# Five of the sixteen column units of the first channel-mix product done in seven block products

## The chip, the cores and the metric

The kernel runs on one core of one Trainium2 chip. The metric is the device time of one execution in microseconds, the median of several runs; lower is better.

## The reference, cut to what matters

The reference is a two-layer encoder trunk on 512 frames of width 1024. The change sits in the channel mix at the end of each layer:

```python
h2 = rmsnorm(x, norm2_g[i])
x = x + jnp.square(jax.nn.relu(h2 @ w_ff1[i] + b_ff1[i])) @ w_ff2[i] + b_ff2[i]
```

`w_ff1` is 1024 x 4096 and `w_ff2` is 4096 x 1024, all in float32. Ahead of it come the combined input projection, two recurrent branches, their merge and the output product `x + merged @ w_out`. Behind it comes the gated per-layer embedding.

## The kernel before, in words

**Products.** Activations lie transposed, features on the 128 partitions and the 512 frames along the free axis. Every float32 operand is split into a high and a low part of type fp32r (`split`: ScalarE copies the high part, VectorE subtracts to get the low part), and a product is three matmuls: high by high, high by low, low by high. `t8` makes one output tile of 128 columns by 512 frames out of eight blocks of the contraction: 24 matmuls, 512 wide.

**Seven products.** A `PAIR` unit is a product of 256 output columns, done as a two-by-two block product in seven block products instead of eight (`run_pair`, `PRODUCTS`). Each of the seven, P1 to P7, is four blocks by three matmuls, 256 wide: 84 matmuls in all. It needs sums of the activation quarters (`operand_sums`, or `pair_operand` for the hidden tiles) and sums of the weight blocks, t1 to t4 (`MADE`). P1 and P5 use the weight piece A, P6 and P2 the piece B, P3 and P7 the piece C, P4 the piece D. P4 of a unit is put off: `later` holds it until `flush`, which stands in the next unit, behind P5 of a pair or behind the fourth block of a `t8`. Before the change the pairs are the retention queries and keys, part of the gates, and the second channel-mix product `w_ff2`; its sixteen units a layer are called `o00` to `o33`.

**Sums of weights.** t1 and t3 are formed in DRAM: `step` issues on GpSimd's queue one copy DMA of 256 KB or one accumulating DMA, and `steps` lists them in the order of `groups`. A credit counter paces them: each unit gives SHARE or LATER times its time, less its loading time (`TIME`), and a step takes STEP = 1.13. A step waits for the last matmul that was written when it was issued (`cur["mm"]`). For the `w_ff2` pairs t2 and t4 are made in SBUF, by two adds of 512 columns on VectorE (L438 and L441).

**Weights on their way.** SyncE loads raw pieces into four buffers (`fill_raws`), and `prep_next` splits them two or so pieces ahead of their product. The order of the instructions on each engine is that of the source, moved by the tile scheduler's priorities; evictions marked `ahead` go first.

**The channel mix.** `ff1(b, p)` makes 256 hidden columns with two `t8` tiles (`f00` to `f33`), multiplies by the norm's factors `n2.b` on VectorE, applies Relu and Square on ScalarE, and forms the quarters' sums. `ff_order` gives the order: f00 f01 f02 f03 f10, o00 to o03, f11 f12 f13 f20, o10 to o13, f21 f22 f23 f30, o20 to o23, f31 f32 f33, an embedding unit, o30 to o33. The norm's factors come from a chain behind f00's first tile: `finish` sums on TensorE, GpSimd raises to the power, `spread` brings the factors to all partitions. Ahead of this stand the eight tiles of `w_out` (`wo`), each followed by a norm tile (`n2.tile`).

Of the kernel before, what the change touches and what calls it, by code (L numbers as in the profile page):

```python
# [42 lines left out]
P = 128  # L43
# [35 lines left out]
def ff_order():  # L79

    seq = [("f", 0, p) for p in range(4)]
    for b in range(3):
# [4 lines left out]

PRODUCTS = {"P1": ("A", 0, 0), "P5": ("A", 1, 4), "P2": ("B", 0, 2), "P6": ("B", 1, 5), "P3": ("C", 0, 6),  # L90
            "P7": ("C", 1, 3), "P4": ("D", 0, 1)}

PIECE = {"A": ("B11", "t1"), "C": ("B22", "t3"), "B": ("B21",), "D": ()}

GIVEN = ("B11", "B12", "B21", "B22")
MADE = {"t1": ("B12", "B11"), "t3": ("B12", "B22"), "t2": ("t1", "B22"), "t4": ("t2", "B21")}
# [8 lines left out]
HALVES = [(WIDE[x][0], u) for x, u in TURNS]  # L105

SOON = ("w_in", 0, CGM + 2 * P)
STEP, SHARE, LATER = 1.13, 0.75, 0.63
TIME = {"PAIR": (9.9, 3.9), "WIDE": (5.45, 2.7)}


def parts_of(u):
# [8 lines left out]
def is_wide(g):  # L121
    return g[1][:2] in ("rv", "rw")


def is_gate(g):
    return g[1][:2] == "rw"


def MADE_OF(g):

    return ("t1", "t3", "t2", "t4") if is_gate(g) else ("t1", "t3", "t2") if is_wide(g) else ("t1", "t3")


def groups():


    g = {}
    for i in range(L):
        def rqk(h):
            return [("w_in", 0, c + k * 256) for k in (h, h + 1) for c in (CRQ, CRK)]  # L140

        g[i, "rv0"] = [("w_in", 0, CRV)]
        g[i, "rqk0"] = rqk(0)
        g[i, "gm"] = [("w_in", 0, CGM + 256 * p) for p in (2, 3)]
        g[i, "rw0"] = [("w_in", 0, CRG)]
        g[i, "rv2"] = [("w_in", 0, CRV + 1024)]
        g[i, "rqk2"] = rqk(2)
        g[i, "rw2"] = [("w_in", 0, CRG + 1024)]
        g[i, "gr"] = [("w_in", 0, CGR + 256 * p) for p in range(4)]
        for b in range(4):  # L150
            g[i, f"ff{b}"] = [("w_ff2", b * 1024, 256 * p) for p in range(4)]
    return g


def unit_list(i):
# [36 lines left out]
    full("w_in", CGM, 0, 2, 3)  # L192
    mqk(2)
    mo(1)
    v(CV + 512)
    mqk(3)
    mo(2)
    full("w_in", CGM, 0, 3, 4)
    mo(3)
    u.append(("WIDE", (i, "rv0"), 0))  # L200
    full("w_bm", 0, 0, 0, 4)
    rqk(0)
    for p in (2, 3):
        pair("gm", p - 2)
        full("w_bm", 0, 0, 2 * p, 2 * p + 2)
    rqk(1)
    u.append(("WIDE", (i, "rw0"), 0))
    u.append(("WIDE", (i, "rv2"), 0))
    rqk(2)
    full("w_br", 0, 0, 0, 4)  # L210
    rqk(3)
    full("w_br", 0, 0, 4, 8)
    u.append(("WIDE", (i, "rw2"), 0))
    for p in range(4):
        pair("gr", p)
        full("w_br", 0, 1024, 2 * p, 2 * p + 2)
    full("w_out")

    def pairs(seq):
        for kind, b, p in seq:  # L220
            if kind == "f":
# [12 lines left out]

def build(ctx, tc, ins, out):
# [120 lines left out]
    def next_unit():  # L356
        n = at["unit"]
        at["unit"] += 1
        tick(units[n][0])
        return n  # L360


    order = [(n, x) for n, u in enumerate(units) for x in parts_of(u)]
    place = {x: k for k, x in enumerate(order)}
    loads = [(n, x) for n, x in order if x != "D" and (x not in (("t4", 0), ("t4", 1)) or is_gate(units[n][1]))]
    raws, pieces, kept = {}, {}, {}
    formed = {}

# [7 lines left out]
    def fill_raws(most=RAWS + 1):  # L376
        while at["load"] < len(loads) and len(raws) + len(kept) < most:
            n, x = loads[at["load"]]
            r = None
            if n in cur["room"] and cur["more"] not in raws:  # L380
                cur["more"] = n, x
                r = cur["low"].tile([P, UN], F32, name=f"wr{at['load']}", tag="wrx", bufs=1)
            elif len(raws) - (cur["more"] in raws) >= RAWS:
                break
            raws[n, x] = r = r or wpool.tile([P, UN], F32, name=f"wr{at['load']}", tag="wr", bufs=RAWS)
            if x:
                _, g, p = units[n]
                assert made.get((g, x[1] if is_wide(g) else p)) == 2 * len(MADE_OF(g)), (g, p, made, at["unit"])
                if is_wide(g):
                    in_order("load", nc.sync.dma_start(r, block(g, x[0])[x[1]]))  # L390
                else:
                    for k, y in enumerate(PIECE[x]):
                        in_order("load", nc.sync.dma_start(r[:, k * Q:(k + 1) * Q], block(g, y)[p]))
            elif units[n][0] == "IF":
                eng = nc.sync if n else nc.scalar
                eng.dma_start(r[:, 0:64], ins["wif"][n * L // NU])
            else:
                w = ins["wstream"][at["whole"]]
                for c in halves(n):
                    in_order("load", nc.sync.dma_start(r[:, c], w[:, c]))  # L400
                at["whole"] += 1
            at["load"] += 1

    def prep_next():
# [24 lines left out]
        else:  # L429
            in_order("prep", *split(r[:, :w], *out_))  # L430
        pieces[n, x] = out_
        if wide and is_gate(units[n][1]):
            pass
        elif x == "A" or wide and x[0] == "t2":
            kept[n, x] = r
# [27 lines left out]
    def t8(act, name):  # L463

        _, wh, wl = unit("T8")
        o = ps(name)
        for k in range(KT):
            s = slice(k * P, (k + 1) * P)
            mm3(o, wh[:, s], wl[:, s], act[0][k], act[1][k], k == 0, k == KT - 1)
            if k == 3:  # L470
                flush()
                pace()
        return o

# [90 lines left out]
    def pair_tiles(name, act, consume, y=None, then=None):  # L565
# [4 lines left out]
        def done(x, o):  # L570
            with ahead():
                evict(x, o)
            if then and x == "P2":
                then()
            if x == "P4":
                consume(y)

# [183 lines left out]
    def values(i, nm, act, rc, bv_ap, n_, mid=None):  # L761
# [4 lines left out]
        for u in range(4):  # L766
# [5 lines left out]
            for kk in range(2):  # L772
                k = 2 * u + kk
                s = slice(kk * T, (kk + 1) * T)
                for j in range(NT):
                    js = slice(j * P, (j + 1) * P)
                    te.matmul(o[j], act[0][k][:, js], wh[:, s], start=(k == 0), stop=False)
                    te.matmul(o[j], act[0][k][:, js], wl[:, s], start=False, stop=False)
                    cur["mm"] = te.matmul(o[j], act[1][k][:, js], wh[:, s], start=False, stop=(k == KT - 1))
        vh = [cur["low"].tile([P, 576], F32R, name=f"{nm}vh{j}", tag="vh", bufs=NT) for j in range(NT)]  # L780
        vl = [cur["low"].tile([P, 576], F32R, name=f"{nm}vl{j}", tag="vl", bufs=NT) for j in range(NT)]
        for j in range(NT):
# [169 lines left out]
    for i in range(L):  # L952
# [160 lines left out]
        def r_attend(h, pt, vv, g=None):  # L1113
# [7 lines left out]
            def each(j):  # L1121
# [2 lines left out]
                c = hv[:, j:j + 1]  # L1124
                gp.tensor_scalar(c, mv[:, j, 1:2], EPS, None, OP.add)
                gp.tensor_tensor(c, c, nhalf[:, 0:1], OP.pow)
                if g and j:
                    r_gate(norm, g, j - 1)

            attend(nm, pt, vv[0], vv[1], 0, 512, num, each)  # L1130
            return norm
# [165 lines left out]
        gs = m_gates(0, xa, n1)  # L1297
        xn_tile(4)
        gm_tile(2, xa, n1)
        xn_tile(5)  # L1300
        m_back(0, gs, num)
        xn_tile(6)
        xn_tile(7)
        xa_pool.release()
        xs_pool = phase(f"xs{i}", act_side)
        shift(xs_pool, act_side, True)
# [50 lines left out]
        yr = acts(cur["br"], f"l{i}yr0")  # L1357
        r_out(0, num[0], yr)
        num = r_attend(1, pt, vv, g)
        r_gate(num, g, NT - 1)  # L1360
        vv = rv_vals(2, lambda: r_out(1, num[0], yr))
        qk = r_qk(2)

# [26 lines left out]

            pair_tiles(f"l{i}gr{p}", xs, consume, then=then)

        gr_gates(0, lambda: r_gate(num, g, NT - 1))
        r_out(3, num[0], yr)
        for c in range(KT):
            if c and c % 2 == 0:
# [26 lines left out]
            gp.dma_start(x[c], x_src[c])  # L1423
        n2_pool = phase(f"n2{i}", act_side)
        n2 = Norm(f"l{i}n2", i, "g2", acts(n2_pool, f"l{i}n2"))
        for c in range(KT):
# [11 lines left out]
        def ff1(b, p):  # L1438
# [5 lines left out]
            def evac(d, o):  # L1444
                a = st[:, d * T:(d + 1) * T]
                ve.tensor_tensor(a, o, n2.b, OP.mult)
                ac.activation(a, a, AF.Relu, bias=bcol(i, "bf1", 8 * b + 2 * p + d))
# [53 lines left out]
        for kind, b, p in first:  # L1501
# [9 lines left out]
            ff1(b, p)  # L1511
        n2_pool.release()
        n3_pool = phase(f"n3{i}", act_side)
        n3 = Norm(f"l{i}n3", i, "g3", acts(n3_pool, f"l{i}n3"))
# [237 lines left out]
```

## Time and profile before

| what | value |
|---|---|
| median of 3 runs | 2329.46 us (2328.98 to 2332.13) |
| the profiled execution | 2331.78 us, span 2330.1 us |
| TensorE | 2313.3 us busy, 99% of the span, granted clock 0.999 |
| VectorE, ScalarE, GpSimd | 1709.6, 1217.6 and 497.2 us busy |
| DMA | 422.15 MB, mean 181 GB/s |

The span runs from the first to the last instruction; the remaining 1.7 us of the execution's time lie around it. The busy time of matmuls is modelled from pipelined records, so how closely matmuls follow each other is read from their start times. A row of the view by windows gives the busy time of each engine in a stretch with its instruction count; a row of the timeline gives start, duration, engine, line, operation and tiles.

### The profile page before, as it was taken

How to read it: one execution, taken by the hardware profiler on the slowest of the kernel's cores; microseconds unless marked ns; L12 is line 12 of the kernel's file. 1: busy time of each engine (PE TensorE's matmuls, PEld its weight loads, DVE VectorE, ACT ScalarE, POOL GpSimd, SP SyncE). 2: the span in 40 equal slices, each digit the busy share in tenths (PEclk: the TensorE clock that was granted, in tenths of full speed). 3: DMA queues.
4: the chain of work that ended last, by engine and by line, in shares of the span. 5: the costliest groups of instructions: out<-in, count | busy, mean ns of one | idle time of the engine just before them, and what ended most of it. 6: DMA issues, size and time to landing. Idle time of an engine off the chain costs nothing.

```text
span 2330.1 us, 34559 instructions
## 1 busy us (share of the span) xinstructions
PE 2313.3 (99%) x12992; PEld 2021.4 (87%) x12992; DVE 1709.6 (73%) x2594; ACT 1217.6 (52%) x1731; POOL 497.2 (21%) x778
## 2 busy tenths in 40 slices
PE   9999999999999999999999999999999999999998
PEld 8888889888888898899888888988888988998997
DVE  7878767886765577678778777778767656776785
ACT  6756434644554445445557564445446445445464
POOL 3222422223123311112422221111121130000012
PEclk9999999999999999999999999999999999999999
DMA  6666997787688776776766668766766852433441
GB/s 202 166 167 157 285 256 212 212 231 212 203 221 231 176 195 174 183 189 177 197 174 168 154 171 233 203 190 193 199 201 185 215 173 96 127 109 96 136 123 55
DMA packets 154121, 422.15 MB, mean 181 GB/s; under 512 B 20880, under 2 KB 24336, under 8 KB 153952
## 3 DMA queue, kind: packets, MB, share of 16 engines
q1 hardware_dynamic: 97504, 257.99, 34.3%
q0 software_dynamic: 41040, 134.51, 26.7%
q10 hardware_dynamic: 15408, 27.43, 3.5%
q8 instruction: 102, 1.67, 0.3%
q14 instruction: 67, 0.55, 0.1%
HBM read 400.97 MB, written 140.51 MB: 232 GB/s over the span
## 4 chain that ended last, share of the span: by engine, by line
PE 90%; DVE 5%; issue 2%; ACT 1%; DMA 1%; POOL 1%; ACTq 0%; DVEq 0%; POOLq 0%; SPq 0%
PE l0f L459 3%; PE l1f L459 3%; PE l1f L460 2%; PE l0f L460 2%; PE l0f L461 2%; PE l1f L461 2%; PE l0br L459 1%; PE l1br L459 1%; PE l1br L460 1%; PE l1br L461 1%; PE l0br L460 1%; PE l0br L461 1%; PE l0pg L459 1%; PE l0bm L459 1%; PE l0pg L460 1%
## 5 line engine op out<-in xcount | busy, mean ns | idle before, releaser
L285 ACT ACTIVATE wh<-wr 128x1024 fp32r<-128x1024 f32 (+1 forms) x223 | 231.5, 1044 | 262.4 <-issue 62.9
L286 DVE TENSOR_TENSOR wl<-wr,wh 128x1024 fp32r<-128x1024 f32 (+1 forms) x221 | 271.8, 1232 | 49.7 <-ACT wh L285 49.3
L285 ACT ACTIVATE wh_B<-wr 128x1024 fp32r<-128x1024 f32 x108 | 114.4, 1059 | 177.2 <-PE l0br L460 15.7
L286 DVE TENSOR_TENSOR wl_B<-wr,wh_B 128x1024 fp32r<-128x1024 f32 x108 | 131.9, 1221 | 51.8 <-ACT wh_B L285 51.7
L459 PE MATMUL l1f<-l1n2h,wh 128*128 128x512 f32 x256 | 99.8, 390 | 0.0
L459 PE MATMUL l0f<-l0n2h,wh 128*128 128x512 f32 x256 | 99.8, 390 | 0.0
L461 PE MATMUL l0f<-l0n2h,wl 128*128 128x512 f32 x256 | 99.7, 389 | 0.0
L461 PE MATMUL l1f<-l1n2h,wl 128*128 128x512 f32 x256 | 99.7, 389 | 0.0
L460 PE MATMUL l0f<-l0n2l,wh 128*128 128x512 f32 x256 | 99.6, 389 | 0.0
L460 PE MATMUL l1f<-l1n2l,wh 128*128 128x512 f32 x256 | 99.6, 389 | 0.0
L285 ACT ACTIVATE wh_D<-wr 128x512 fp32r<-128x512 f32 x60 | 37.9, 632 | 113.1 <-DVE wr L441 49.2
L285 ACT ACTIVATE wh_C<-wr 128x1024 fp32r<-128x1024 f32 x60 | 63.4, 1056 | 61.5 <-issue 8.3
L285 ACT ACTIVATE wh_t<-wr 128x1024 fp32r<-128x1024 f32 x56 | 59.4, 1060 | 66.8 <-PE l1g2va L554 6.0
L286 DVE TENSOR_TENSOR wl_t<-wr,wh_t 128x1024 fp32r<-128x1024 f32 x56 | 68.1, 1219 | 25.9 <-ACT wh_t L285 25.2
L286 DVE TENSOR_TENSOR wl_C<-wr,wh_C 128x1024 fp32r<-128x1024 f32 x60 | 74.8, 1247 | 16.3 <-ACT wh_C L285 15.8
L285 ACT ACTIVATE wh_A<-wr 128x1024 fp32r<-128x1024 f32 x60 | 63.1, 1052 | 40.8 <-PE l1f L460 6.7
L286 DVE TENSOR_TENSOR wl_A<-wr,wh_A 128x1024 fp32r<-128x1024 f32 x60 | 73.2, 1221 | 12.0 <-ACT wh_A L285 11.4
L673 POOL TENSOR_TENSOR l1n3sum<-l1n3sum,l1n3sq 128x512 f32<-128x512 f32 x6 | 9.3, 1546 | 330.7 <-ACT l1n3sum L665 309.8
L286 DVE TENSOR_TENSOR wl_D<-wr,wh_D 128x512 fp32r<-128x512 f32 x60 | 41.4, 690 | 25.7 <-ACT wh_D L285 24.5
L461 PEld LDWEIGHTS l0f<-l0n2h,wl 128*128 128x128 f32 x256 | 48.1, 188 | 10.2
L461 PEld LDWEIGHTS l1f<-l1n2h,wl 128*128 128x128 f32 x256 | 48.1, 188 | 10.1
L460 PEld LDWEIGHTS l0f<-l0n2l,wh 128*128 128x128 f32 x256 | 48.1, 188 | 9.8
(4990 smaller groups left out, 8428.5 us busy)
## 6 DMA issues: line engine op xcount, KB each, us to landing
wr<-wstream SPq DMA_DIRECT2D x219, 512.0 KB, 4.4
wr<-wpairs SPq DMA_DIRECT2D x180, 256.0 KB, 3.5
wr<-wwide SPq DMA_DIRECT2D x48, 512.0 KB, 4.5
s3t<-wwide POOLq DMA_DIRECT2D x24, 256.0 KB, 5.5
s6t<-wwide POOLq DMA_DIRECT2D x24, 256.0 KB, 4.9
s15t<-wwide POOLq DMA_DIRECT2D x24, 256.0 KB, 4.4
s18t<-wwide POOLq DMA_DIRECT2D x24, 256.0 KB, 4.1
s0t<-wwide POOLq DMA_DIRECT2D x20, 256.0 KB, 4.1
```

The lines of the kernel that those rows point to most:

```text
L285: a = ac.activation(hi_ap, src, AF.Copy)
L286: return a, ve.tensor_sub(lo_ap, src, hi_ap.bitcast(F32))
L459: te.matmul(o, sh, mh, start=first, stop=False)
L460: te.matmul(o, sh, ml, start=False, stop=False)
L461: cur["mm"] = te.matmul(o, sl, mh, start=False, stop=last)
L673: (add or gp).tensor_tensor(self.sum, self.sum, sq, OP.add)
```

## The change

Five of the sixteen `ff1` units of each layer, f11, f13, f21, f23 and f31, become `PAIR` units of new groups `fp1`, `fp2` and `fp3`. The operand sums that they need (`n2_seven`) are formed behind every second tile of the output product `w_out`, in a new pool of 16 tiles. The weight sum t2 of all channel-mix pairs, old and new, is formed in DRAM in both layers, and t4 too in layer 1, so the adds at L438 go in both layers and those at L441 in layer 1; piece B is then two loads, and piece D of layer 1 is a load. That makes 630 steps on GpSimd's queue where there were 464 (each layer gains 32 or 64 for `w_ff2` and 30 or 40 for the new groups). LATER rises from 0.63 to 0.73, and `pace` is called at two places of a `t8` instead of one and after each `V` unit. Besides, two gate steps of the retention branch move later by one place and three norm tiles (`xn_tile`) earlier.

```diff
+FPAIRS = ((1, 1), (1, 3), (2, 1), (2, 3), (3, 1))
-PIECE = {"A": ("B11", "t1"), "C": ("B22", "t3"), "B": ("B21",), "D": ()}
+PIECE = {"A": ("B11", "t1"), "C": ("B22", "t3"), "B": ("B21", "t2"), "D": ("t4",)}
-STEP, SHARE, LATER = 1.13, 0.75, 0.63
-TIME = {"PAIR": (9.9, 3.9), "WIDE": (5.45, 2.7)}
+STEP, SHARE, LATER = 1.13, 0.75, 0.73
+TIME = {"PAIR": (9.9, 3.9), "WIDE": (5.45, 2.7), "FULL": (9.9, 5.0)}
+def is_full(g):
+    return is_gate(g) or g[0] > 0 and g[1][0] == "f"
+def has_t2(g):
+    return is_full(g) or g[1][0] == "f"
...
+            f = [p for c, p in FPAIRS if c == b]
+            if f:
+                g[i, f"fp{b}"] = [("w_ff1", 0, b * 1024 + 256 * p) for p in f]
             g[i, f"ff{b}"] = [("w_ff2", b * 1024, 256 * p) for p in range(4)]
...
-        if wide and is_gate(units[n][1]):
+        if full(n) or not wide and x in ("A", "C") and has_t2(units[n][1]):
             pass
...
             if k == 3:
                 flush()
+            if k in (2, 5):
                 pace()
...
-                if g and j:
-                    r_gate(norm, g, j - 1)
+                if g and j > 1:
+                    r_gate(norm, g, j - 2)
...
-        xn_tile(5)
+        for k in (5, 6, 7):
+            xn_tile(k)
         m_back(0, gs, num)
-        xn_tile(6)
-        xn_tile(7)
...
-        gr_gates(0, lambda: r_gate(num, g, NT - 1))
+        gr_gates(0, {"P6": lambda: r_gate(num, g, 2), "P2": lambda: r_gate(num, g, 3)})
...
+        def n2_sums(k):
+            v = [tmp(f"l{i}ns{k}{a}") for a in range(2)]
+            for a in range(2):
+                ve.tensor_tensor(v[a], *[t[2 * k + a].bitcast(F32) for t in n2.act], OP.add)
+            operand_sums(f"l{i}ns{k}", v, *[t[2 * k:2 * k + 2] for t in ns])
         for c in range(KT):
             o = t8((mh, ml), f"l{i}wo{c}")
             ve.tensor_tensor(x[c], o, x[c], OP.add)
             n2.tile(c, x[c])
+            if c % 2:
+                n2_sums(c // 2)
...
+            if (b, p) in FPAIRS:
+                def consume(y):
+                    for d in range(2):
+                        evac(d, y[d], SIGN[d])
+                    pair_quarters(st, *hid[b, p])
+                    pair_operand(nm, st, *hid[b, p])
+                pair_tiles(nm, n2_seven, consume, [st[:, d * T:(d + 1) * T] for d in range(2)])
+                return
```

Where the rows below name `wh` and `wl`, these are the high and the low part of a split weight piece (`wh_A` of piece A of a pair, without a letter of a `t8`), `st` is a unit's staging tile, `hl` the low part of its hidden tiles.

On VectorE in layer 0, around unit f11, there stood before:

```order
L1446 TENSOR_TENSOR l0f11st<-l0f_8593,l0n2rb 128x512
L286 TENSOR_TENSOR wl_0_8639<-wr_8487,wh_0_8638 128x1024
L1446 TENSOR_TENSOR l0f11st<-l0f_8642,l0n2rb 128x512
L286 TENSOR_TENSOR wl_0_8684<-wr_8564,wh_0_8683 128x1024
L599 TENSOR_TENSOR l0f11st<-l0f11st 128x512
L600 SCALAR_TENSOR_TENSOR l0f11st<-l0f11st 128x256
L286 TENSOR_TENSOR l0hl_8584<-l0f11st,l0hh_8583 128x768
L601 SCALAR_TENSOR_TENSOR l0f11st<-l0f11st 128x256
```

Now there stands, from the eviction of its product P2 on:

```order
L606 TENSOR_TENSOR l0f11st<-l0f11b,l0f11st 128x256
L304 TENSOR_TENSOR wl_0_8827<-wr_8698,wh_0_8826 128x1024
L610 TENSOR_TENSOR l0f11st<-l0f11c,l0f11st 128x256
L612 TENSOR_TENSOR l0f11st<-l0f11a,l0f11st 128x256
L1485 TENSOR_TENSOR l0f11st<-l0f11st,l0n2rb 128x512
L304 TENSOR_TENSOR wl_A<-wr_8721,wh_A 128x1024
L1485 TENSOR_TENSOR l0f11st<-l0f11st,l0n2rb 128x512
L621 TENSOR_TENSOR l0f11st<-l0f11st 128x512
L1485 TENSOR_TENSOR l0f12st<-l0f_8853,l0n2rb 128x512
L304 TENSOR_TENSOR l0hl_8718<-l0f11st,l0hh_8717 128x768
L622 SCALAR_TENSOR_TENSOR l0f11st<-l0f11st 128x256
L304 TENSOR_TENSOR wl_C<-wr_8744,wh_C 128x1024
```

Three evictions of 256 columns are new, the multiplications by the norm's factors read SBUF instead of the accumulator, and pieces A and C of the next pair, f13, are split among f11's own steps.

On VectorE in layer 0, two tiles of the output product took these rows before:

```order
L1428 TENSOR_TENSOR l0x_7328<-l0wo_7370,l0x_7328 128x512
L286 TENSOR_TENSOR wl_0_7404<-wr_7228,wh_0_7403 128x1024
L655 SCALAR_TENSOR_TENSOR l0n2l_7348<-l0x_7328,bc,l0n2h_7347 128x512
L1428 TENSOR_TENSOR l0x_7329<-l0wo_7407,l0x_7329 128x512
L286 TENSOR_TENSOR wl_0_7443<-wr_7287,wh_0_7442 128x1024
L655 SCALAR_TENSOR_TENSOR l0n2l_7350<-l0x_7329,bc,l0n2h_7349 128x512
```

After the last of these rows there stands now:

```order
L1460 TENSOR_TENSOR l0ns_7503<-l0n2h_7390,l0n2l_7391 128x512
L1460 TENSOR_TENSOR l0ns_7504<-l0n2h_7392,l0n2l_7393 128x512
L633 TENSOR_TENSOR l0ns0u_7507<-l0ns_7503 128x256
L634 TENSOR_TENSOR l0ns0u_7507<-l0ns_7504,l0ns_7503 128x256
L635 SCALAR_TENSOR_TENSOR l0ns0u_7508<-l0ns0u_7507,l0ns_7503 128x256
L636 SCALAR_TENSOR_TENSOR l0ns0u_7508<-l0ns0u_7508,l0ns_7504 128x256
L304 TENSOR_TENSOR l0nsl_7417<-l0ns0u_7507,l0nsh_7409 128x512
L1465 TENSOR_TENSOR l0x_7373<-l0wo_7524,l0x_7373 128x512
```

The operand sums of two tiles add eight VectorE rows (the eighth, a second `nsl` of 512 columns, stands a little further on) ahead of and behind the next tile's addition to `x`.

On GpSimd in layer 1, ahead of the norm's power `l1n2rc`, there stood only the norm's own additions; now steps of the weight sums (`s27t`) stand between them:

```order
L361 DMA s27t_174<-s27t_172 64x1024 x2
L361 DMA s27t_174<-wpairs 64x1024
L695 TENSOR_TENSOR l1n2sum<-l1n2sum,l1n2sq_19383 128x512
L361 DMA s27t_174<-wpairs 64x1024 x3
L709 TENSOR_TENSOR l1n2rc<-l1n2ms,nhalf 128x4
L361 DMA s27t_175<-s27t_174 64x1024 x4
```

Layer 1's queue now looks here as layer 0's did before, where steps stood ahead of `l0n2rc` already.

More of the change, by code (lines that the diff above doesn't have):

```diff
@@ L129, in MADE_OF @@
 def MADE_OF(g):
-    return ("t1", "t3", "t2", "t4") if is_gate(g) else ("t1", "t3", "t2") if is_wide(g) else ("t1", "t3")
+    return ("t1", "t3", "t2", "t4") if is_full(g) else ("t1", "t3", "t2") if is_wide(g) or has_t2(g) else ("t1", "t3")
 def groups():
@@ L220, in pairs @@
         for kind, b, p in seq:
-            if kind == "f":
+            if (b, p) in FPAIRS and kind == "f":
+                pair(f"fp{b}", [q for c, q in FPAIRS if c == b].index(p))
+            elif kind == "f":
                 t8("w_ff1", b * 1024 + 256 * p)
@@ L358, in next_unit, with full @@
         at["unit"] += 1
-        tick(units[n][0])
+        tick("FULL" if full(n) and units[n][0] == "PAIR" else units[n][0])
         return n
+    def full(n):
+        return units[n][0] in ("PAIR", "WIDE") and is_full(units[n][1])
     order = [(n, x) for n, u in enumerate(units) for x in parts_of(u)]
     place = {x: k for k, x in enumerate(order)}
-    loads = [(n, x) for n, x in order if x != "D" and (x not in (("t4", 0), ("t4", 1)) or is_gate(units[n][1]))]
+    loads = [(n, x) for n, x in order if full(n) or x not in ("D", ("t4", 0), ("t4", 1))]
     raws, pieces, kept = {}, {}, {}
@@ L391, in fill_raws @@
                 else:
-                    for k, y in enumerate(PIECE[x]):
+                    for k, y in enumerate(PIECE[x][:1] if x == "B" and not has_t2(g) else PIECE[x]):
                         in_order("load", nc.sync.dma_start(r[:, k * Q:(k + 1) * Q], block(g, y)[p]))
@@ L572, in done @@
                 evict(x, o)
-            if then and x == "P2":
-                then()
+            if then and x in then:
+                then[x]()
             if x == "P4":
@@ L779, in values @@
                     cur["mm"] = te.matmul(o[j], act[1][k][:, js], wh[:, s], start=False, stop=(k == KT - 1))
+                pace()
         vh = [cur["low"].tile([P, 576], F32R, name=f"{nm}vh{j}", tag="vh", bufs=NT) for j in range(NT)]
@@ L1359, in build @@
         num = r_attend(1, pt, vv, g)
-        r_gate(num, g, NT - 1)
+        for j in (2, 3):
+            r_gate(num, g, j)
         vv = rv_vals(2, lambda: r_out(1, num[0], yr))
@@ L1425, in build @@
         n2 = Norm(f"l{i}n2", i, "g2", acts(n2_pool, f"l{i}n2"))
+        ns_pool = phase(f"ns{i}", act_side)
+        if i == L - 1:
+            ns = [a.bitcast(F32R) for a in big(f"l{i}nsh", F32)]
+        else:
+            ns = [ns_pool.tile([P, T], F32R, name=f"l{i}nsh{k}", tag="nh", bufs=KT) for k in range(KT)]
+        ns = ns, [ns_pool.tile([P, T], F32R, name=f"l{i}nsl{k}", tag="nl", bufs=KT) for k in range(KT)]
+        n2_seven = sevenfold(n2.act, ns)
+        def n2_sums(k):
[3 more added lines that the diff above has]
+            operand_sums(f"l{i}ns{k}", v, *[t[2 * k:2 * k + 2] for t in ns])
         for c in range(KT):
@@ L1442, in ff1, with evac @@
             st = cur["ff"].tile([P, 8 * S], F32, name=nm + "st", tag="st", bufs=2)
[L1444 removed]
+            def evac(d, o, sign=1.0):
                 a = st[:, d * T:(d + 1) * T]
                 ve.tensor_tensor(a, o, n2.b, OP.mult)
[L1447 removed]
+                ac.activation(a, a, AF.Relu, bias=bcol(i, "bf1", 8 * b + 2 * p + d), scale=sign)
                 ac.activation(a, a, AF.Square)
+            if (b, p) in FPAIRS:
[6 more added lines that the diff above has]
+                return
             o = t8(n2.act, f"{nm}0")
@@ L1511, in build @@
             ff1(b, p)
+        ns_pool.release()
         n2_pool.release()
```

## The prediction

> **What bounds the kernel now.** I read the page's first parts, then TensorE's waits, then the windows of the stages that the change touches.
>
> ```profile
> PE 2313.3 (99%) x12992; PEld 2021.4 (87%) x12992; DVE 1709.6 (73%) x2594; ACT 1217.6 (52%) x1731; POOL 497.2 (21%) x778
> PEclk9999999999999999999999999999999999999999
> ```
>
> TensorE is busy 99% of the span at its full granted clock. So either its work shrinks or nothing much can be won. Its waits say the same; these are the longest, in total us, times, longest:
>
> ```profile
> PE l0r0brqa L509 <- DVE l0r0brqy L590: 1.7, 1, 1.7
> ...
> PE l0gr0a L509 <- ACT l0gr0y L580: 0.8, 1, 0.8
> PE l1m2z L460 <- DVE l1xnl L286: 0.8, 1, 0.8
> PE l1gr0a L509 <- ACT l1gr0y L580: 0.6, 1, 0.6
> ...
> PE l0o30a L511 <- DVE wl_B L286: 0.3, 1, 0.3
> PE l1o30a L511 <- DVE wl_B L286: 0.3, 1, 0.3
> ```
>
> Nothing else of size is waited for. The stages, in the order output product, first five ff1 units, four ff2 pairs, a long mixed stretch of the channel mix, the first part of layer 1; each row has length, TensorE, its weight loads, VectorE, ScalarE and GpSimd busy, clock, DMA share, GB/s:
>
> ```profile
> 726.30:769.80 43.50, 43.50 (x193) 36.04 (x192) 21.87 (x26) 17.07 (x23) 19.00 (x19) 1.00 0.73 192
> 769.80:825.70 55.90, 55.90 (x252) 46.34 (x251) 37.05 (x53) 30.53 (x39) 14.19 (x19) 1.00 0.71 174
> 825.70:866.00 40.30, 40.22 (x333) 39.70 (x332) 35.10 (x56) 18.81 (x21) 5.71 (x9) 1.00 0.69 194
> 866.00:1065.70 199.70, 199.67 (x1207) 178.60 (x1206) 141.02 (x201) 97.03 (x117) 34.51 (x53) 1.00 0.69 179
> 1235.00:1880.00 645.00, 643.24 (x3525) 557.77 (x3524) 484.35 (x749) 340.27 (x515) 135.53 (x228) 1.00 0.70 195
> ```
>
> VectorE is the second engine: idle half the time in the output product, but busy 35.1 of 40.3 us in the pairs. DMA has 0.7 of its time taken.
>
> **The change part by part. TensorE.** The first row above is eight `t8` tiles in 43.5 us, 5.44 us each. A pair's pitch stands in two rows of the timeline, the first matmul of P1 and the first of P5, twelve matmuls later:
>
> ```profile
> 825.92 0.28 PE L509 MATMUL l0o00a<-l0hh,wh_A 128*128 128x256 f32 x1
> 827.33 0.28 PE L509 MATMUL l0o00c<-l0hh,wh_A 128*128 128x256 f32 x1
> ```
>
> A product takes 1.41 us, so seven take 9.87 where two tiles took 10.88: 1.01 us a unit, 10.1 for ten units. The order agrees that nothing else is added: 360 matmuls more, ten times 84 less 48. A matmul 256 wide takes 117.5 ns, one of 512 wide 226.7, so halving the width costs 4%; this is already in the 9.87. The Trainium skill ("TensorE: Matmul & The Clock Gate", section Back-to-back issue gap) speaks against such a change: its sustained spacing for streams of weight load and matmul is about 81 ns at 128 columns and 131 at 512. Between these I would put about 98 ns at 256, an estimate, and a pair would take 8.2 us against 6.3 for two tiles, 19 us lost over ten units. The trace does not agree with these spacings, and it decides.
>
> **Stalls that go.** The gate steps moved by one place stand before the `gr0` waits, the norm tiles moved forward before `l1m2z`, and the adds that go (L438 twice over, L441 in layer 1) before `o30`. The rows above offer 0.8 + 0.6 + 0.8 + 0.6 = 2.8 us; I take 2.0, between nothing and 2.8, nearer the upper end since each is a VectorE or ScalarE instruction in front of the waited one.
>
> **VectorE.** The prices, from the page and the timeline:
>
> ```profile
> L286 DVE TENSOR_TENSOR wl_B<-wr,wh_B 128x1024 fp32r<-128x1024 f32 x108 | 131.9, 1221 | 51.8 <-ACT wh_B L285 51.7
> L286 DVE TENSOR_TENSOR wl_D<-wr,wh_D 128x512 fp32r<-128x512 f32 x60 | 41.4, 690 | 25.7 <-ACT wh_D L285 24.5
> 799.52 1.22 DVE L286 TENSOR_TENSOR l0hl<-l0f01st,l0hh 128x1024 fp32r<-128x1024 f32 x1
> 800.66 1.22 DVE L286 TENSOR_TENSOR wl<-wr,wh 128x1024 fp32r<-128x1024 f32 x1
> 807.09 0.68 DVE L599 TENSOR_TENSOR l0f02st<-l0f02st 128x512 f32<-128x512 f32 x1
> 807.70 0.95 DVE L286 TENSOR_TENSOR l0hl<-l0f02st,l0hh 128x768 fp32r<-128x768 f32 x1
> 808.56 0.42 DVE L600 SCALAR_TENSOR_TENSOR l0f02st<-l0f02st 128x256 f32<-128x256 f32 x1
> 835.07 0.41 DVE L1475 TENSOR_TENSOR l0x<-l0x,l0o00b 128x256 f32<-128x256 f32 x1
> ```
>
> A pair in ff1 costs splits 3 x 1.22 + 0.69, evictions 3 x 0.41, two multiplications at 0.69 (nearest row: wl_D, 512 columns out of SBUF), and the hidden operand 0.68 + 0.95 + 2 x 0.42 + 1.22 = 3.69: 10.65 us, in layer 0 another 0.69 for the sum at L441. That is over its 9.87 on TensorE. But instructions in a row overlap: the two 1.22 rows start 1.14 apart, and at such a pitch the sum is about 9.7. And the double tile beside it costs only 2.44 + 1.38 + 3.69 = 7.5 of 10.88, so that a pair and a double tile ask 18.2 of 20.75. Hidden, then, but without room to be late. What is queued behind: the second multiplication of f11 waits for P4, which comes only four blocks into f12's first tile; behind it stand pieces C and B of f13 and behind those f13's evictions. Walking the rows of the order at these pitches from f11's start, piece B of f13 is split at 24.2 us and wanted at 25.0; f13's operand is done at 43.1 and wanted by o10's P5 at 44.4; piece B of o10 at 44.8, wanted at 45.8. These margins of about 1 us are estimates. A lateness of 0.2 us at three places, twice a layer, would be 2.4 us in all; with 0 as the other end I take 1.6. The pairs of ff2 gain room: one add of 0.69 less of some 8.8 in layer 0, two in layer 1.
>
> In the output product the operand sums add 4 x (4 x 0.69 + 4 x 0.42) = 17.8 us to 21.87 of 43.5: 39.7, hidden, and read only at f11. The norm chain behind it has this slack:
>
> ```profile
> 776.49 0.16 DVE L684 TENSOR_SCALAR l0n2ms<-l0n2ss 128x4 f32<-128x4 f32 x1 [2.82 <-PE l0n2ss L680]
> 780.09 0.61 DVE L729 SCALAR_TENSOR_TENSOR l0n2dl<-ident,l0n2rc,l0n2dh 128x128 fp32r<-128x128 f32 x2
> L731 PE MATMUL l0n2rp<-l0n2dh,ones_r x1: 403/403/403, 781.9 to 781.9; 128*128 128x512 f32 x1
> ```
>
> The last four rows of sums fall into VectorE's 2.82 us idle, or push `n2dl`, which ends at 780.7, by about 0.6; TensorE asks for it at 781.9. Zero; without this slack 0.6 a layer.
>
> **ScalarE.**
>
> ```profile
> L285 ACT ACTIVATE wh_A<-wr 128x1024 fp32r<-128x1024 f32 x60 | 63.1, 1052 | 40.8 <-PE l1f L460 6.7
> 643.21 0.36 ACT L580 ACTIVATE l0gr0y<-l0gr0a 128x256 f32<-128x256 f32 x1
> ```
>
> It is busy 30.5 of 55.9 us in the first ff1 units, about 6 us a unit, and a pair gives it 1.5 pieces more (1.6 us) and four copies of 256 columns (1.4): 9 of 9.87 us, with the lighter double tiles between. Hidden; no term, and the same rival as VectorE's if it is not.
>
> **GpSimd and DMA.** 166 steps of 0.262 MB are 43.5 MB more on the software queue, and loads grow by 48 blocks for ff2 and 25 for ff1, 19.1 MB.
>
> ```profile
> q1 hardware_dynamic: 97504, 257.99, 34.3%
> q0 software_dynamic: 41040, 134.51, 26.7%
> 232.00:349.00 117.00, 115.19 (x643) 100.25 (x642) 83.34 (x124) 52.82 (x80) 40.50 (x63) 1.00 0.94 269
> 311.13 5.94 DMA wr<-s2t
> ```
>
> By the first two rows a MB takes 4.63 us of all engines on the software queue and 3.10 on the other. The credit lets (0.73 x 5.45 - 1.5) / 1.13 = 2.19 steps go with a `t8` and (0.73 x 9.9 - 3.9) / 1.13 = 2.94 with a pair of layer 0. Beside a `t8` that is 1.63 for its load of 0.524 MB and 2.19 steps at 1.21, 4.3 of 5.44: a share of 0.79 where 0.71 is measured. Beside a pair it is six loads, 4.88, and 3.57 for the steps: 0.86 of 9.87. The stretch from 232 to 349 us already runs at 0.94, and TensorE misses 1.8 of its 117 us, all of it by the one late piece in the last row, which made the 1.7 us wait of `l0r0brqa`. So 0.86 costs nothing; if that cover is gone, 1.7 us a late piece. The steps on GpSimd's queue pass the norm's power in layer 1 now, as they did in layer 0, where no wait for it is shown: zero. The last step is issued in layer 1's channel mix, so the loads that use it are still well behind it.
>
> **The sum.** From the profiled execution's 2331.8 (span 2330.1 and 1.7 around it): -10.1 - 2.0 + 1.6 = -10.5, 2321.3. That execution is 2.3 us above the median of the three runs; on the median the forecast is 2319.0. A measurement can tell 0.2%, 4.7 us, from no change.
>
> **The rivals.**
>
> VectorE falls behind in ff1. The 1 us margins are missed, and every pair loses 0.5 us (the rows of `o30` show 0.3 for a late wl_B), five over the ten, 2324. For it: a pair asks 10.65 us of VectorE for 9.87. Against it: VectorE idles in the tiles beside, and its queue takes pieces two ahead. 12%.
>
> Weights come late because the DMA engines are full; this ends slower. In layer 0's channel mix 21 pairs draw 0.86 by my sum. If bursts of steps fill the engines and one piece per pair comes late at the 1.7 us of `l0r0brqa`, 36 us are lost, 2355, and at half of the pairs 18 us, 2337; from the seventh late piece on the gain of 10.5 is gone. For it: 166 more steps and a faster pace. Against it: a share of 0.94 made one such wait in 117 us. 8%.
>
> A narrow matmul costs its weight load. In the trace a load takes as long for a narrow as for a wide matmul:
>
> ```profile
> L509 PEld LDWEIGHTS l0o00a<-l0hh,wh_A x4: 188/188/188, 825.7 to 826.9; 128*128 128x128 f32 x4
> ```
>
> If the loads were the bound, 84 x 0.188 = 15.8 us a pair, 4.9 more than two tiles, 2368. The pitch of 117.5 ns refutes it for ff2's pairs, and the new ones have the same form. The sustained spacing of the page named above falls under this rival too. 1%.
>
> That the change does not do what it says is ruled out by the order's 360 matmuls; no chance of its own.
>
> **How the numbers follow.** The forecast has 79%: its own range is from 2316.0 (10.1 and all 2.8 of stalls won, nothing lost, rounded down) to 2322 (no stall won, 2.4 lost). The range reaches up to 2325 and takes in the VectorE rival; the DMA rival and the narrow matmul are left out. Faster by over 0.2%, below 2324.8: the forecast and a part of the first rival, 84%. Within 0.2%: the rest of it and the mildest of the DMA rival, 8%. Slower: 8%.
>
> **What would show it.** In the new profile f11's products should start 1.41 us apart, TensorE's matmuls number 360 more, and busy VectorE in the stretch from f11 to f20 should be near 90%. The waits of TensorE for `gr0` and `m2z` should be gone. Right: TensorE's waits stay under 12 us in all. Wrong: waits of TensorE for wl_A, wl_B or wl_C of f11 to f31 and o10 to o30 summing to over 5 us (VectorE), waits of those splits for DMA with a share over 0.95 in layer 0's channel mix (DMA), or a pitch above 117.5 ns in f11.

## The result, and the profile after

The changed kernel takes 2323.05 us (median of 11 runs, 2320.34 to 2326.78), the kernel before, timed beside it, 2329.25 us (11 runs, 2328.45 to 2333.25). The ratio is 0.997 with a 95% interval from 0.9963 to 0.9978: 6.2 us less, between 5.1 and 8.6. The forecast was 10.3 to 10.5 us less, 2319.0 in a range from 2316.0 to 2325.0. The sign and the mechanism held; the gain came out some 40% smaller than forecast.

The profiled execution of the changed kernel took 2324.59 us (span 2322.9), 7.2 us under the one of before. The page's busy times, then the first rows of TensorE's waits (engine, line, who is waited for: us in total, times, longest), then two of the DMA queues (packets, MB, share):

```profile
PE 2306.3 (99%) x13352; PEld 2033.3 (88%) x13352; DVE 1752.4 (75%) x2665; ACT 1257.8 (54%) x1807; POOL 600.4 (26%) x944
```
```profile
PE l1r0brqa L531 <- DVE l1r0brqy L612: 1.7, 1, 1.7
PE l0r0brqa L531 <- DVE l0r0brqy L612: 1.6, 1, 1.6
...
PE l0gr0a L531 <- DVE l0gr0y L612: 0.6, 1, 0.6
PE l1gr0a L531 <- DVE l1gr0y L612: 0.6, 1, 0.6
```
```profile
q1 hardware_dynamic: 110896, 277.13, 35.8%
q0 software_dynamic: 54320, 178.04, 35.4%
```

TensorE has 360 matmuls more and 7.0 us less to do (2313.3 before). The wait of `l1m2z` is gone from the list. The `gr0` waits are still there, with VectorE's `gr0y` as releaser where ScalarE's was. The first row is new: layer 1's `l1r0brqa` had no such wait before. GpSimd's queue carries 43.5 MB more, as worked out.

By stages (length, then TensorE, its weight loads, VectorE, ScalarE, GpSimd busy, clock, DMA share, GB/s), the windows view of the changed kernel for the output product, the first five `ff1` units, the two stretches from `o03` to `o10` and from `o13` to `o20` (an `ff2` pair and four `ff1` units, two of them new pairs), and the last stretch, with one new pair:

```profile
725.88:769.42 43.54, 43.54 (x194) 36.04 (x192) 38.40 (x50) 20.75 (x30) 20.45 (x24) 1.00 0.82 216
769.42:825.27 55.85, 55.85 (x251) 46.33 (x250) 39.99 (x60) 31.67 (x42) 15.81 (x24) 1.00 0.78 205
853.99:907.30 53.31, 53.31 (x362) 49.49 (x361) 38.96 (x56) 32.21 (x45) 11.26 (x17) 1.00 0.81 216
936.33:989.63 53.30, 53.30 (x362) 49.47 (x361) 38.65 (x56) 32.21 (x45) 11.40 (x18) 1.00 0.83 227
1018.64:1061.83 43.19, 43.19 (x278) 39.41 (x277) 30.32 (x43) 24.27 (x33) 9.09 (x14) 1.00 0.83 220
```

The same view of the kernel before, for the third and the fifth of these:

```profile
854.63:909.53 54.90, 54.90 (x291) 47.36 (x289) 34.74 (x46) 26.35 (x33) 9.68 (x15) 1.00 0.70 183
1021.88:1065.90 44.02, 44.02 (x242) 38.34 (x241) 27.74 (x38) 21.09 (x27) 7.85 (x12) 1.00 0.69 178
```

The first two stages cost what they cost before (43.50 and 55.90, cut a little differently), with VectorE's sums of 16.5 us hidden in the first. Two new pairs save 54.90 - 53.31 = 1.59 us, one saves 0.83: 0.80 a pair. Layer 1 gives the same numbers (1.58, 1.58, 0.83), so all ten save 8.0 us. The rest of the 7.2 is a balance of +0.8: the stretch from `m2z` to `m3z` is 1.46 shorter in both layers together and `gr0` 0.35, against 1.96 at `l1r0brqa` and a net 0.7 in small pieces. Among these the 0.3 us waits at `o30` went, too: from `o30` to `o31` TensorE's first matmuls were 9.02 us apart in both layers and are now 8.75 and 8.74; but from `o33` to `pg` it is 0.37 and 0.64 us longer. These are the two rows of layer 1's `m2z` stretch, before and after:

```profile
1274.73:1339.21 64.48, 63.71 (x305) 53.09 (x304) 47.61 (x88) 35.49 (x59) 15.09 (x34) 1.00 0.61 151
```
```profile
1270.54:1333.93 63.39, 63.39 (x305) 53.18 (x304) 47.33 (x87) 35.08 (x58) 19.23 (x40) 1.00 0.71 178
```

**Why 0.80 and not 1.01 a pair.** The timeline of TensorE in f11 of the changed kernel, the first matmuls of P6, P2 and P3:

```profile
868.17 0.29 PE L531 MATMUL l0f11a<-l0nsh,wh_B 128*128 128x256 f32 x1
869.62 0.28 PE L531 MATMUL l0f11b<-l0n2h,wh_B 128*128 128x256 f32 x1
871.06 0.28 PE L531 MATMUL l0f11c<-l0nsh,wh_C 128*128 128x256 f32 x1
```

A product takes 1.45 and 1.44 us, a pitch of 120.4 ns, not the 117.5 ns taken from one product of `o00`. Seven such are 10.1 us, and 10.88 - 10.1 is the 0.8 measured. The product of `o00` was no exception among the `ff2` pairs. These are the first matmuls of `o02` and `o03` in the kernel before, a whole pair apart:

```profile
844.74 0.28 PE L509 MATMUL l0o02a<-l0hh,wh_A 128*128 128x256 f32 x1
854.63 0.28 PE L509 MATMUL l0o03a<-l0hh,wh_A 128*128 128x256 f32 x1
```

That is 9.89 us for 84 matmuls, 117.7 ns each, and the changed kernel has the same 9.89 us there. So the new pairs are slower than the pairs of `ff2`, all ten of them alike (119.8 to 120.0 ns from start to start). What differs is the moving operand: the norm's tiles `n2` and their sums `ns` here, the hidden tiles there. The kernel before showed such a difference already, within one pair of the gates, whose products read either the norm's tiles `xn` or their sums `xs`; these are the first matmuls of P6, P2 and P3 of `gr2`:

```profile
687.54 0.28 PE L509 MATMUL l0gr2a<-l0xsh,wh_B 128*128 128x256 f32 x1
688.95 0.29 PE L509 MATMUL l0gr2b<-l0xnh,wh_B 128*128 128x256 f32 x1
690.39 0.28 PE L509 MATMUL l0gr2c<-l0xsh,wh_C 128*128 128x256 f32 x1
```

P6 on `xs` takes 1.41 us, P2 on `xn` 1.44. Two of the experiments move the operands.

**The late load.** Layer 1 from 1440 us on, before and then after, by windows:

```profile
1440.00:1460.00 20.00, 20.00 (x90) 16.54 (x89) 10.77 (x14) 5.40 (x6) 3.95 (x6) 1.00 0.74 193
1460.00:1475.00 15.00, 15.00 (x119) 14.61 (x118) 9.18 (x12) 6.45 (x10) 3.15 (x5) 1.00 0.79 220
```
```profile
1440.00:1460.00 20.00, 20.00 (x102) 17.08 (x101) 9.01 (x10) 4.63 (x5) 5.49 (x9) 1.00 0.90 239
1460.00:1475.00 15.00, 13.30 (x112) 13.10 (x112) 8.81 (x14) 7.39 (x13) 2.64 (x4) 1.00 0.85 209
```

The chain of waits of the changed kernel passes here through a load, and the timeline of VectorE shows who stood for it:

```profile
1461.46 6.09 DMA wr<-wpairs
```
```profile
1467.67 0.69 DVE L459 TENSOR_TENSOR wr<-wr,wr 128x512 f32<-128x512 f32 x1 [4.15 <-DMA wr<-wpairs]
1468.28 0.42 DVE L610 TENSOR_TENSOR l1r0brqy<-l1r0brqc,l1r0brqy 128x256 f32<-128x256 f32 x1
```

The load takes 6.09 us, VectorE idles 4.15 us for it at the add of two weight blocks, and the evictions of `l1r0brqy` stand behind that add; TensorE then waits 1.7 us for an accumulator. In the kernel before VectorE idled 1.23 us at the same add and TensorE not at all.

### The profile page after: what moved, and what is told of

It is laid out like the page before. It is cut to its first block, busy times and chain, and to the rows that moved or that the text cites. A ratio compares the mean times of both kernels' runs of the same rounds, so it can differ in the third digit from the quotient of the medians.

```text
span 2322.9 us, 35908 instructions
## 1 busy us (share of the span) xinstructions
PE 2306.3 (99%) x13352; PEld 2033.3 (88%) x13352; DVE 1752.4 (75%) x2665; ACT 1257.8 (54%) x1807; POOL 600.4 (26%) x944
## 4 chain that ended last, share of the span: by engine, by line
PE 90%; DVE 5%; issue 2%; DMA 1%; ACT 1%; POOL 1%; DVEq 0%; ACTq 0%; SPq 0%; POOLq 0%
PE l1f L480 2%; PE l1f L481 2%; PE l1f L482 2%; PE l0br L480 1%; PE l1br L480 1%; PE l1br L481 1%; PE l0br L481 1%; PE l1br L482 1%; PE l0br L482 1%; PE l0f L480 1%; PE l0f L481 1%; PE l0f L482 1%; PE l0pg L480 1%; PE l1bm L480 1%; PE l0bm L480 1%
## 5 line engine op out<-in xcount | busy, mean ns | idle before, releaser
L303 ACT ACTIVATE wh<-wr 128x1024 fp32r<-128x1024 f32 (+1 forms) x203 | 210.3, 1042 | 154.3 <-issue 22.1
L304 DVE TENSOR_TENSOR wl<-wr,wh 128x1024 fp32r<-128x1024 f32 (+1 forms) x201 | 245.6, 1224 | 38.5 <-ACT wh L303 38.3
L480 PE MATMUL l1f<-l1n2h,wh 128*128 128x512 f32 x176 | 68.7, 390 | 0.0
L480 PE MATMUL l0f<-l0n2h,wh 128*128 128x512 f32 x176 | 68.7, 390 | 0.0
L481 PE MATMUL l0f<-l0n2l,wh 128*128 128x512 f32 x176 | 68.6, 390 | 0.0
L481 PE MATMUL l1f<-l1n2l,wh 128*128 128x512 f32 x176 | 68.6, 390 | 0.0
L482 PE MATMUL l0f<-l0n2h,wl 128*128 128x512 f32 x176 | 68.5, 389 | 0.0
L482 PE MATMUL l1f<-l1n2h,wl 128*128 128x512 f32 x176 | 68.5, 389 | 0.0
L482 PEld LDWEIGHTS l0f<-l0n2h,wl 128*128 128x128 f32 x176 | 33.0, 188 | 7.0
L480 PEld LDWEIGHTS l0f<-l0n2h,wh 128*128 128x128 f32 x176 | 33.1, 188 | 6.6
```

Of the source, the lines that this page charges most:

```text
L303: a = ac.activation(hi_ap, src, AF.Copy)
L304: return a, ve.tensor_sub(lo_ap, src, hi_ap.bitcast(F32))
L480: te.matmul(o, sh, mh, start=first, stop=False)
L481: te.matmul(o, sh, ml, start=False, stop=False)
L482: cur["mm"] = te.matmul(o, sl, mh, start=False, stop=last)
```

## The experiments

**No new pair, the rest of the change kept.** Timed in five rounds.

```diff
-FPAIRS = ((1, 1), (1, 3), (2, 1), (2, 3), (3, 1))
+FPAIRS = ()
```

> The changed kernel with no ff1 unit in seven products; its operand sums after the output product are still formed, though read by nothing, and t2 and t4 of the ff2 pairs are still made in DRAM, the gate steps and norm tiles moved. Theory A (each of the ten pairs is worth 0.80 us, 8.0 in all, and the rest of the change nets +0.9 us): 2330 us, 0 to 1.5 above the kernel before; the stretches from o03 to o10 back at 54.90. Theory B (a pair is worth 1.01 and the steps and splits that come with the pairs take back 3 us elsewhere): 2327 to 2328, below the kernel before by some 2 us, with the wait of l1r0brqa gone since there are 70 fewer steps.

2330.34 us against 2328.53, ratio 1.0006 (0.9997 to 1.0015). Without the pairs the change gains nothing: +1.8 us, between -0.7 and +3.5. With the pairs it is -6.2, so that ten pairs are worth about 8.0 us on the clock as well, the 0.80 each of the stages. The two figures are from different sessions, each against its own runs of before, so this is good to some 2 us. The steps of the new groups are left out with the pairs, 70 fewer, and the new wait nearly goes; theory B had expected it gone:

```profile
PE l1r0brqa L531 <- DVE l1r0brqy L612: 0.4, 1, 0.4
```

**The moved gates and norm tiles alone,** on the kernel before. Five rounds.

```diff
-                    r_gate(norm, g, j - 1)
+                    r_gate(norm, g, j - 2)
...
-        xn_tile(5)
+        for k in (5, 6, 7):
+            xn_tile(k)
...
-        gr_gates(0, lambda: r_gate(num, g, NT - 1))
+        gr_gates(0, {"P6": lambda: r_gate(num, g, 2), "P2": lambda: r_gate(num, g, 3)})
```

> The kernel before with only the moved calls of the change: the gates' work of the stages gr and m2z is issued two products later, and the mixing of xn's last tiles earlier; no pair of seven products. Theory A (the waits read from the two traces are all that these moves are worth): the m2z wait goes in both layers (stage m2z to m3z shorter by 0.4 and 1.1 us), gr0's falls by 0.1 to 0.25 us in each layer, in all 1.5 to 2 us: about 2327.5 us, ratio 0.9992. Theory B (what the moves gain at m2z comes back as waits for the later stages' weights or at r0brqa, as the kernel without the pairs left it open: 2330.3 against 2328.5): 2329 to 2331 us, and stage lengths after m3z longer by 1.5 us or more in all.

Of the norm tiles the edit, like the change, moves two: `xn_tile(5)` stood ahead of `m_back` already. 2328.95 us against 2327.65, ratio 1.0003 (0.9994 to 1.0011): between -1.4 and +2.6 us. This is its stretch from `l1m2z` to `l1m3z`, 63.39 us where before had 64.48, and layer 1's `gr0` in its list of waits, with the releaser of the changed kernel:

```profile
1271.36:1334.75 63.39, 63.39 (x305) 53.17 (x304) 46.80 (x86) 34.62 (x57) 16.09 (x34) 1.00 0.59 150
```
```profile
PE l1gr0a L509 <- DVE l1gr0y L590: 0.6, 1, 0.6
```

The `m2z` wait is gone; the median does not show the 1.5 to 2 us that its stages promise. Neither theory is shown: 0.9992 lies just outside the interval, and no later stage is 1.5 us longer in its profile. One profile of before says what that execution waited, and this wait may be shorter in others; that is argued, not shown.

**The summed operands at another offset.** By the program's allocation the tiles `n2`, `ns` and `xn` start 224 bytes past a multiple of 256 bytes, the sums `xs` and the hidden tiles 32 bytes past one; `shift` moves what is allocated behind it from the one to the other. One profiled execution.

```diff
         ns_pool = phase(f"ns{i}", act_side)
+        shift(ns_pool, act_side, True)
...
+        shift(ns_pool, act_side, False)
```

> The changed kernel with the operand sums of the new pairs placed 64 or 192 bytes further on, as the kernel already places the retention's sums (offset 32 instead of 224 within 256 bytes; in layer 1 only the low parts, since the high parts lie in a shared buffer). Theory A: the pitch of a 256-wide matmul depends on where its moving operand starts: the products on sums (P5, P6, P3, P7) of f11 in layer 0 go from 1.44 to 1.41 us, those on the norm's own tiles (P1, P2, P4) stay at 1.44, and the stretch from o03 to o10 in layer 0 goes from 53.31 to about 53.1 us; layer 1 gains a third of that, 0.6 to 0.8 us in all. Theory B: the pitch comes from two operands lying in separate tiles, or from the weights' side: no product changes, the stretch stays at 53.3.

2319.71 us in the one run. The timeline of TensorE in f11, the first matmuls of the same three products:

```profile
866.74 0.28 PE L531 MATMUL l0f11a<-l0nsh,wh_B 128*128 128x256 f32 x1
...
868.16 0.29 PE L531 MATMUL l0f11b<-l0n2h,wh_B 128*128 128x256 f32 x1
...
869.60 0.28 PE L531 MATMUL l0f11c<-l0nsh,wh_C 128*128 128x256 f32 x1
```

The product on the moved sums takes 1.42 us, 118 ns a matmul; the one on the unmoved `n2` stays at 1.44, 120 ns. Each of the stretches with two pairs in layer 0 becomes 0.17 us shorter. That is the size that theory A gave, but its reason holds only half: in layer 1 the high parts lie in an older buffer, which the edit did not move, and the pitch on them fell just the same (120.1 to about 118 ns in the timed repeat below). So the placement of the operands sets the pitch, not simply each operand's own offset.

**Both operands of n moved.** One profiled execution.

```diff
+        shift(n2_pool, act_side, True)
+        shift(n2_pool, act_side, False)
```

> The changed kernel with the norm's tiles n2 shifted, and with them the sums that lie behind them, to offset 32. Theory A (the start of the moving operand sets the pitch): all seven products of f11 in layer 0 at 1.41 us, the pair at 9.87, the stretch from o03 to o10 of layer 0 at about 52.9 instead of 53.31; whether the 512-wide tiles of ff1 gain too (5.44 us now, also at offset 224) is open; if their matmuls also lose 2.5 ns, eleven double units a layer gain 1.3 us a layer, and f00 to o00 goes from 55.85 to about 55.2. Theory B (separate tiles, or the weights): nothing changes.

2322.31 us in the one run. These are the first matmuls of P6, P2 and P3 of `f21` in layer 0:

```profile
948.41 0.28 PE L531 MATMUL l0f21a<-l0nsh,wh_B 128*128 128x256 f32 x1
...
949.83 0.28 PE L531 MATMUL l0f21b<-l0n2h,wh_B 128*128 128x256 f32 x1
...
951.24 0.28 PE L531 MATMUL l0f21c<-l0nsh,wh_C 128*128 128x256 f32 x1
```

Both products now take 1.41 to 1.42 us, 117.8 ns a matmul, the pace of the `ff2` pairs. So the placement of the operands is what made the new pairs slower. (`f11` and `f13` run at 113.3 ns in this execution; so do `o02` and `o03` ahead of them, which is a spell as described at the end.) But the 512-wide tiles on the same operands get slower, as the windows of the first five units in both layers show:

```profile
768.65:824.97 56.32, 56.32 (x251) 46.34 (x250) 39.96 (x60) 31.68 (x42) 15.81 (x24) 1.00 0.81 204
1918.31:1974.63 56.32, 56.32 (x251) 46.34 (x250) 39.92 (x60) 31.69 (x42) 16.18 (x24) 1.00 0.73 186
```

56.32 where 55.85 stood, 0.47 us over some 250 matmuls, nearly 2 ns each. `n2` feeds both widths, so moving it wins nothing.

**No background steps at the late load.** Units 180 to 183 are layer 1's from `bm` to the pairs of `r0`. One profiled execution.

```diff
-        if at["step"] < len(steps) and at["credit"] >= 0:
+        if at["step"] < len(steps) and at["credit"] >= 0 and at["unit"] not in HOLD:
...
+    HOLD = range(180, 184)
...
+        if at["unit"] in HOLD:
+            return
```

> The changed kernel with no step of the weight sums issued, and no credit given, while units 180 to 183 of the program's list run (layer 1's last two bm tiles and the first two pairs of queries and keys). Theory A (l1r0brqa waits 1.7 us since steps on the same engines make the load of the next pair's weights take 6.1 us): that load lands in under 4.5 us, the wait is under 0.3 us, and the stretch from l1r0brqa to l1bgm2a goes from 20.49 back to about 18.5. Theory B (the load comes late because its buffer comes free late, whatever the steps do): the wait stays at 1.7.

2321.39 us in the one run. The same two windows, then the first rows of TensorE's waits:

```profile
1440.00:1460.00 20.00, 20.00 (x114) 17.59 (x114) 8.94 (x10) 5.97 (x9) 0.00 (x0) 1.00 0.38 126
1460.00:1475.00 15.00, 15.00 (x128) 15.00 (x128) 12.34 (x20) 7.37 (x12) 2.66 (x5) 1.00 0.53 180
```
```profile
PE l1o10a L535 <- DVE l1x L1527: 1.1, 1, 1.1
PE l0r0brqa L535 <- DVE l0r0brqy L616: 1.1, 1, 1.1
```

The DMA share falls from 0.90 and 0.85 to 0.38 and 0.53, TensorE does not stop, and the stretch to `l1bgm2a` is 18.53 us long instead of 20.49, the length it had before. So the steps made that load late. But a new wait of 1.1 us stands at `o10` of layer 1, far behind the units without steps.

**Repairs, timed.** The held steps, the moved sums, and both together, five rounds each on one chip beside before (2327.65 us).

> The changed kernel with no background step in units 180 to 183, timed. Theory A: the wait of 1.7 us at layer 1's r0brqa is gone again, and the waits at o10 of layer 1 give back 0 to 1.2 us: 2321 to 2322.5 us. Theory B (what is held back is paid in full later): 2323 us, with new waits of 1.5 us or more in the units after 184.

> The kernel of the first look at the offset, timed: only the summed operands of n moved to 32 bytes into a 256-byte line. Theory A (the offset sets the pitch): the products on these operands 117.9 ns a matmul instead of 120.0 again, about 0.17 us for each four stages f11 to f20, 0.5 to 1 us in all, 2322 to 2322.8 us. Theory B (a spell of that execution): pitch 120 ns again and 2323 us.

> The changed kernel with both repairs: the summed operands of n start 32 bytes into a 256-byte line as those of x do, and no background step is issued in units 180 to 183. Theory A (pitch by the operand's offset, and the late load by the steps' traffic): 0.5 us from the pitch and 1.96 us from the load, less at most 1.2 us for a wait that the held steps bring at o10 of layer 1: 1.3 to 2.5 us under the changed kernel, 2320.5 to 2322 us. Theory B (the held steps' traffic is late wherever it is put, and the pitch of the single look was a spell of that execution): within 1 us of the changed kernel, 2322 to 2324 us.

Held steps: 2320.87 us, ratio 0.9969 (0.9958 to 0.9981). Moved sums: 2320.78, 0.9971 (0.996 to 0.9982). Both: 2320.02, 0.997 (0.9958 to 0.9981). All three stand where the changed kernel itself stood, 0.997. So the changed kernel and the version with both repairs were timed side by side, five rounds each:

> The changed kernel itself, unaltered, timed beside the version with both repairs on one chip. Theory A: 6.2 us under before again (ratio 0.9973), and 1.5 to 2.5 us over the version with the repairs. Theory B (the repairs' gains are within the spread of executions): within 1 us of the version with the repairs. In its profile, the wait at layer 1's r0brqa of 1.7 us should stand again by both if it is a matter of the program, and the short spells in which a stage of products runs 0.7 us faster should lie elsewhere than before.

> The version with both repairs once more, beside the changed kernel. Theory A: 1.5 to 2.5 us faster than the changed kernel on the same chip; 0.9964 of before. Theory B: no difference of 1 us.

2321.87 us (0.997, 0.9958 to 0.9981) against 2321.67 (0.9968, 0.9956 to 0.998); before 2328.62. The medians are 0.2 us apart, as theory B said; with six runs each, spread over 3 to 4 us, the 1.5 us of theory A is not ruled out. The profiles show where the repair went. First the changed kernel's wait in this execution, then the version with both repairs, its longest wait and a piece of its chain of waits before it:

```profile
PE l1r0brqa L531 <- DVE l1r0brqy L612: 1.2, 1, 1.2
```
```profile
PE l1o10a L535 <- DVE l1x L1529: 1.2, 1, 1.2
```
```profile
2035.84 6.83 DMA wr<-s25t
...
2042.78 1.07 ACT wh_A L303
2043.85 0.02 issue
2043.87 1.23 DVE wl_A L304
...
2056.50 1.13 DVE wl_B L304
2057.63 0.34 DVE l1x L1529
```

A load of 6.83 us again, of a piece for f13. ScalarE's and VectorE's work on f13 runs late behind it, then the split of `o10`'s piece B, and behind that the eviction that frees the accumulator. A late load now stands some 580 us further on and costs the same 1.2 us. A wait at `o10` of layer 1 was in all four profiles with held steps, and none at `l1r0brqa`; in the five with the ten pairs and no hold it was the reverse, `l1r0brqa` waiting 1.2 to 1.9 us. That the held steps bring the second wait is therefore shown. How they do is not: they run later from unit 184 on, but the seven microseconds of this load have a DMA share of 0.87 where the changed kernel's same stretch has 0.92 without the wait.

## Why the prediction was right, and where it was off

- **The pairs' worth** was the step that failed: -10.1 forecast, -8.0 measured. The mechanism is right: seven products for eight, and what TensorE saves shows in the stages. The term was mis-sized. I took the pitch of a product of `o00`, 117.5 ns, and held that "the new ones have the same form". The pitch was right for `ff2`, 9.89 us a pair, but it did not carry over: on `n2` and `ns`, placed as they are, a matmul starts every 120 ns, a pair takes 10.1 us, and ten pairs save 8.0. In the kernel before the products of `gr2` on `xn` had shown the 1.44 us.
- **Stalls that go:** -2.0 forecast. The profile gives -1.8 (`m2z` 1.46, `gr0` 0.35), but nearly all of it at `m2z` and not at `gr0`, where the wait stayed and only its releaser changed. The two waits at `o30` went as forecast, 0.55 us between them, and are in the small pieces. The moves by themselves gave no gain that the timing shows (-1.4 to +2.6 us).
- **VectorE:** +1.6 forecast, about +0.6 found, all of it in layer 0 at the first matmuls of o10's and o20's P6 (0.3 us each). The margin at piece B of `o10` was forecast at 1 us; the split ended at 909.94 us and TensorE wanted it at 910.14, then started at 910.41, behind the eviction that follows the split on VectorE. So the queue was the right place to look. The load on VectorE was overestimated: near 90% forecast from f11 to f20, 31.24 of 43.42 us (72%) measured.

```profile
863.88:907.30 43.42, 43.42 (x278) 39.60 (x277) 31.24 (x44) 28.50 (x41) 9.17 (x14) 1.00 0.79 212
```

- **Output product, norm chain, ScalarE:** zero forecast, zero measured: 43.54 and 55.85 us.
- **DMA:** zero forecast, one late load found that costs 1.2 to 1.9 us, in layer 1 and not where the rival looked for it. The shares came out as worked out beside the `t8` tiles (0.79 forecast, 0.78 measured) and in the channel mix (0.86 forecast beside a pair and 0.79 beside a tile, 0.81 to 0.83 in the stretches that mix them). The reason given, that 0.94 cost one late piece in 117 us and so 0.86 would cost nothing, was too simple: a 6.09 us load came at 0.85. The rival's mechanism occurred once, at its price of 1.7 us, and so it did not decide.
- **VectorE behind in every pair** (2324 us) came near the median by its number, but not by its cause: the waits it needs sum to 0.6 us, not 5.
- **The narrow matmul that costs its weight load** did not come: 120 ns a matmul against a load of 188. Its price was off as well: ten times 4.9 us more than two tiles counts from the kernel before, not from the forecast that holds the gain already, so it is some 2378 us and not 2368.
- **The range and the signs.** 2323.05 us lies above the forecast's own range, 2316.0 to 2322, and inside the stated one only because that was widened to 2325 for the VectorE rival, whose cause did not come; to that extent it was luck. Of the signs, the 360 matmuls, the `m2z` wait that goes and waits under 12 us (8.9 in the list) came. The `gr0` waits and the 90% of VectorE did not, and a pitch above 117.5 ns in `f11`, which the prediction named as a sign of being wrong, is what was found.
- **The sum** with the terms as the profiles show them: -8.0 - 1.8 + 1.96 + 0.7 = -7.1, near the -7.2 between the two profiled executions and inside the measured -5.1 to -8.6.

## What to carry to other kernels

Price a new unit from one that reads the same operands, or operands placed alike, and not only from one of the same form: the `ff2` pair took 9.89 us, the new pair 10.1, and at a gain of one us a pair that is a fifth of it. Holding background traffic back at one late load can bring a wait of the same size elsewhere, so look at the whole list of waits and not at the one that went. And where repairs are worth 1 to 2 us, read them in the stages of more than one profile, and believe the gain only when the timing beside the unrepaired kernel shows it.

## What the runs showed that I had not expected

**Placement and pitch.** With the moving operands 224 bytes past a multiple of 256 a 256-wide matmul starts every 120 ns, and every 118 ns when they are moved to 32 bytes past one. The 512-wide ones on the same operand go the other way, by some 2 ns. Why is open: in layer 1 the unmoved high parts gained too.

**Spells.** The same instructions take two lengths in different executions, at a granted clock of 1.00 in both. These are the three pairs from `o10` to `o13` of layer 0 in the kernel before and in the kernel with only the moves, whose code is the same here:

```profile
909.53:938.25 28.72, 28.71 (x241) 28.41 (x240) 26.32 (x42) 14.02 (x16) 4.45 (x7) 1.00 0.68 183
```
```profile
908.18:936.18 28.00, 27.88 (x241) 27.58 (x240) 26.14 (x42) 14.03 (x16) 4.45 (x7) 1.00 0.68 184
```

0.72 us apart, with the same DMA share; in `o12` a matmul starts every 117.8 ns in the first and every 113.3 in the second. The changed kernel shows it too: 29.03 us in one execution and 28.19 in the other. The spells take in one or more of the blocks of `ff2` pairs, other blocks in each execution, and the 512-wide tiles between them keep their pace. The two profiles compared stage by stage above, of before and of the changed kernel, have none: all whole `ff2` pairs in them keep 117 to 118 ns. The profiles of other executions have them, so a total read from one profile can be off by some 2 us, an estimate from two or three blocks at 0.7 to 0.8 us. Their cause was not found.
